# Hybrid decoder layer with 32 experts: w2 in packets of 16 KB, and three pieces of work moved

## The chip, the cores and the metric

The kernel runs on one core of a Trainium2 chip. Times are device microseconds of one execution, from launch to end; lower is better. The engines are PE (matrix products; PEld are its weight loads), DVE, ACT and POOL (work on vectors), and SP, which here only issues transfers.

## The reference

One layer on 256 rows of 1024 numbers, all in float32. First a mixing stage (a projection, differential attention beside an RWKV recurrence, an output projection), then a mixture of experts; each stage has its norms and takes shift, scale and gate from a conditioning vector. The attention needs a scalar `lambda` from four short vectors. The experts:

```python
logits = tok @ router_w + router_b
top_vals, top_idx = lax.top_k(logits, TOP_K)          # 4 of 32
gates = sum(one_hot(top_idx, 32) * softmax(top_vals)[..., None], axis=1)
...
out = clamped_swiglu(tok @ w1_e + b1_e) @ w2_e + b2_e   # w1_e 1024 x 2048, w2_e 1024 x 1024
acc = acc + g_e[:, None] * out                          # over all 32 experts
```

`clamped_swiglu` takes even and odd columns of its input as gate and linear part. All 32 experts' weights, 12 MB each, have to be read.

## The kernel before

The program is one function, in which the order of PE, DVE and ACT is mostly written out (under `manual_schedule`).

**Start (to about 60 us).** x is normed and transposed (`x_tr`), the shift and scale of the first 256 features come from two products of the conditioning vector with pieces of `ada_w` (`mod_rows`, copied by `mod_copy`, turned into columns by `mod_cols_first`), and `mod_x` makes the normed rows as a sum of two parts, high and low. `col_tr(0)` transposes small parameter rows into the columns `pc`. Seven matmuls with a tile of zeros clear the seven banks into which the first projection (`proj_first`) then accumulates. `warm(n)` issues n matmuls on ones whose result nobody reads. `shift` applies the token shift behind the projection. Lambda is four vectors' products, a sum, an Exp and a difference (L729 to L736). SP issues the loads in the order of the code; the table of the experts' first biases, `b1q` (128 rows of 512), is the last of `load_later` (L229) and is read by four matmuls and two splits about 230 us into the run.

**Middle (to about 240 us).** Attention, recurrence, output projection and router, in an order given by the string `WORK`.

**Experts (loop at L1923).** The experts are taken in an order by their number of rows; each has room for 64, 32 or 96 (`kind`). For expert p, `gemm1` (L1709) does 8 k-steps: the selected rows `xs[:, k]` are stationary, and 512 columns at a time of w1 move through PE, two or four streams in different column groups of PE (`parts`, L1684). `swiglu` makes `act` (DVE and ACT), `act_tr` transposes it, ACT copies it as `aTt`, and `gemm2` (L1736) does 8 k-steps with w2, each with a number of rows per partition. ACT and DVE evacuate the result as `ys`, and `scatter` (L1776) puts it back to the 256 rows by a product with the selection `back`; DVE adds it into `acc`. Work on the next expert (`gather`, `prep_back`, `gemm1_bias`) and the scatter of the previous one stand between these steps, some of it inside `gemm2` by the dictionary `between`, whose keys are k.

**Weights.** A ring of 18 slots of 1 MB holds them; an expert takes 8 for w1 and 4 for w2. `load_expert` (L1577) is a generator: one `next` behind each k-step of gemm1 issues a piece of the next expert, on SP's queue. w1 goes in four transfers of 2 MB, 16 KB (two rows) per partition, w2 in four of 1 MB, 8 KB (two rows) per partition, in the order `W2_ORDER`. The first four experts (`single`) take all of it in 1 MB.

**Last expert.** It has no successor. Its `between` (L1969) puts the scatter of the previous expert and `sum_so_far` (L1764: identity times `acc`, and the gates times the second biases `b2t`, into the four banks `ends`) into its gemm2, and 24 warm-up matmuls stand ahead of the transposes. The last `scatter` adds into `ends`, and `last_norm` and the output follow. `late_rows` (L1852) has POOL load the second biases at the start of the last expert.

Of the kernel before, what the change touches and what calls it, by code (L numbers as in the profile page):

```python
# [20 lines left out]
D = 1024  # L21
# [28 lines left out]
WARM = (34, 4, 0, 6, 8)  # L50
# [25 lines left out]
def hybrid_layer_kernel(ctx, tc, x, c, positions, ada_w, ada_b, pre_mix_norm, post_mix_norm,  # L76
# [146 lines left out]
    def load_later():  # L223
        for j, ap in enumerate((lam_q1, lam_k1, lam_q2, lam_k2)):
            nc.sync.dma_start(lamt[:, j], bcast(ap, [[0, 128], [1, 64]]))
        nc.sync.dma_start(rtw.rearrange("p (j r) e -> p j r e", r=2), router_w[0].rearrange(
            "(j p r) e -> p j r e", p=128, r=2))
        nc.sync.dma_start(rtb, router_b)
        nc.sync.dma_start(b1q, moe_b1[0].rearrange("e (q n) -> (e q) n", q=4))  # L229
# [68 lines left out]
    load_cols(0, S, ((("sh1", "sc1"), ada_b[0, 0:2 * D]), (("pre_mix",), pre_mix_norm[0])))  # L298
    ident = const.tile([128, 128], F32)
    V.tensor_scalar(ident, jp, 0.0, None, op0=OP.is_equal)  # L300

# [111 lines left out]
    norm_x(xj)  # L413
    x_tr(0, xj[0])
    mod_rows(0, 0, ada)
    x_tr(1, xj[1])
    mod_rows(0, 1, ada)
    col_tr(0)
# [8 lines left out]
    rwb = {}  # L427
    ORDER = (0, 2, 4, 6, 8, 10, 12)
    for f in ORDER:
        rwb[f] = (bankb if f in (12, 8, 10) else bank)()  # L430
        mm(rwb[f], zero, zero[:, 0:1].to_broadcast([128, 512]), True, False)
    warm(WARM[1], bankc)
# [11 lines left out]

    def shift(dst, p, f):
        S.activation(dst, p, AF.Copy, scale=mu1[:, f:f + 1])  # L446
        V.scalar_tensor_tensor(dst[:, 1:], p[:, 0:T - 1], col("mu", f), dst[:, 1:], op0=OP.mult, op1=OP.add)  # L447
# [281 lines left out]
    V.tensor_tensor(lamt[:, 0], lamt[:, 0], lamt[:, 1], op=OP.mult)  # L729
    V.tensor_tensor(lamt[:, 2], lamt[:, 2], lamt[:, 3], op=OP.mult)  # L730
    V.tensor_reduce(lam2, lamt[:, 0:4:2], axis=AX.X, op=OP.add)
    with tc.issue_after(first_act.ins):
        S.activation(lam2, lam2, AF.Exp)
    nlam = pro.tile([128, 1], F32)
    V.tensor_tensor(nlam, lam2[:, 1:2], lam2[:, 0:1], op=OP.subtract)
    V.tensor_scalar(nlam, nlam, LAMBDA_INIT, None, op0=OP.subtract)  # L736
# [416 lines left out]
    rkr, gB = rT, gT  # L1153
    fill()
# [422 lines left out]
    def load_expert(e, s1_, s2_, single=False):  # L1577


        w1 = moe_w1[0][e] if isinstance(e, int) else moe_w1[0][bass.ds(e, 1)].rearrange("o k n -> (o k) n")  # L1580
        w2 = moe_w2[0][e] if isinstance(e, int) else moe_w2[0][bass.ds(e, 1)].rearrange("o k n -> (o k) n")
        at = taken[0]
        taken[0] += KC + 4
        for j in range(4):

            d = ring[(at + 2 * j) % N_SLOTS // 2]
            s = w1[j * 256:(j + 1) * 256, :].rearrange("(p k) n -> p k n", k=2)
            s1_ += [d[:, 0], d[:, 1]]
            if j == 3:
                yield  # L1590
            if single:
                nc.sync.dma_start(d[:, 0], s[:, 0])
            if j == 3:
                yield
            if single:
                nc.sync.dma_start(d[:, 1], s[:, 1])
            else:
                nc.sync.dma_start(d.rearrange("p k n -> p (k n)"), s.rearrange("p k n -> p (k n)"))
        for n, k in enumerate(W2_ORDER):
            yield  # L1600
            s = s2_[k] = slot((at + KC + n) % N_SLOTS, (2, D))
            nc.sync.dma_start(s, w2[k * 256:(k + 1) * 256, :].rearrange("(p k) n -> p k n", k=2))
# [80 lines left out]

    def parts(bs, kind):  # L1684
        if kind != 32:
            for n in range(2):
                for h in range(2):
                    yield bs[n][64 * h:64 * h + 64], slice(0, 64), h * 1024 + n * 512
        if kind != 64:
            for q in range(4):  # L1690
                yield bs[-1][32 * q:32 * q + 32], slice(kind - 32, kind), q * 512
# [17 lines left out]
    def gemm1(bs, xs, w1s, kind, between=None, load=None):  # L1709
        for k in range(KC):  # L1710
            for o, s, c0 in parts(bs, kind):
                mm(o, xs[:, k, s], w1s[k][:, c0:c0 + 512], False, k == KC - 1)
# [21 lines left out]
    W2_ORDER = (0, 2, 1, 3)  # L1734

    def gemm2(aTt, w2s, gates_of, kind, between=None):  # L1736

        ks = [2 * s + j for s in W2_ORDER for j in range(2)]
# [37 lines left out]
    def scatter(ys, back, which=range(NT)):  # L1776
# [146 lines left out]
    for p in range(EXPERTS):  # L1923
        kind = kind_at(p)
        w1s, w2s = weights
        if p + 1 < EXPERTS:
            weights = [], {}
            rest_of_load = load_expert(expert_of(p + 1), *weights, p + 1 < SINGLE)
# [12 lines left out]
        if p + 1 < EXPERTS:  # L1941
# [16 lines left out]
            between[5] = lambda: back1.append(prep_back(nxt[1], gate1, kind1, picked(p + 1)))  # L1958
        back1 = []
        if p == 0:  # L1960
# [6 lines left out]
            between[3], between[5] = between[5], rest_of_first  # L1967
# [20 lines left out]
    scatter(*done[:2])  # L1988
# [67 lines left out]
```

## Time and profile before

| | us |
|---|---|
| three runs, lowest, median, highest | 1188.75, 1189.94, 1190.77 |
| the profiled execution, its own time | 1190.35 |
| its span, from first to last instruction | 1188.5 |
| PE busy in the span | 1078.3 (91%) |
| DVE, ACT busy | 412.1 (35%), 227.6 (19%) |
| DMA: moved, mean rate | 453.15 MB, 381 GB/s |
| mean granted clock of PE, as a share of full | 0.972 |

1.85 us of the execution lie outside the span. In the profile a busy PE may be waiting on its operands within a matmul; matmul ends are modelled. A row of a timeline is a start, a duration, engine and line, operation, what it writes <- what it reads, shape, count, and in brackets the idle time of its engine before it with what released it. Names are the program's, without numbers: `pair` is a slot of the ring (or, early on, a buffer in the same place), `bank`, `bankb`, `bankc` are accumulators. Line 104 is the helper behind every matmul, so matmuls are told apart by tiles. The chain of work that ended last is 45% transfers (44% weights of the experts) and 45% PE.

### The profile page before, as it was taken

The numbers are of one execution on the slowest core, as the hardware profiler recorded it, in microseconds if no ns is written. First come the engines' busy times: TensorE is split into PE (matmuls) and PEld (weight loads), VectorE is DVE, ScalarE is ACT, GpSimd is POOL, SyncE is SP. The second block draws the span as 40 slices with busy tenths as digits, with TensorE's granted clock in tenths as the row PEclk, the third lists the DMA queues.
The fourth block names the chain that finished last, engine by engine and source line by source line (L and its number), as shares of the span: only waits on it lengthen the run. The fifth ranks groups of instructions, "written<-read, shape, count | busy, mean of one in ns | idle before, by whom it ended". The sixth has DMA issues, their size and how long they took to land.

```text
span 1188.5 us, 17092 instructions
## 1 busy us (share of the span) xinstructions
PE 1078.3 (91%) x6717; PEld 507.3 (43%) x6717; DVE 412.1 (35%) x1114; ACT 227.6 (19%) x529; POOL 53.7 (5%) x100
## 2 busy tenths in 40 slices
PE   8999999999997877999988999988999999798765
PEld 6976667654343232233443233433333434333211
DVE  5688469852331212122323112312212223121203
ACT  4374353312011001010111010111010101101001
POOL 1331020000000000000000000000000000000000
PEclk8999999999999988999999999999999999999978
DMA  9862778899999999999999999999999999999991
GB/s 336 317 235 71 280 270 330 326 371 383 423 424 426 426 425 426 425 426 424 425 425 426 424 426 427 422 426 426 423 426 426 425 426 425 425 426 425 423 382 48
DMA packets 60101, 453.15 MB, mean 381 GB/s; under 512 B 7850, under 2 KB 16105, under 8 KB 23154
## 3 DMA queue, kind: packets, MB, share of 16 engines
q1 hardware_dynamic: 57970, 449.88, 91.9%
q0 software_dynamic: 1856, 2.13, 0.6%
q8 instruction: 54, 0.88, 0.3%
q14 instruction: 29, 0.24, 0.1%
q10 hardware_dynamic: 192, 0.02, 0.0%
HBM read 450.94 MB, written 1.06 MB: 380 GB/s over the span
## 4 chain that ended last, share of the span: by engine, by line
DMA 45%; PE 45%; DVE 6%; ACT 2%; issue 1%; SPq 0%; DVEq 0%; ACTq 0%
DMA pair<-in_moe_w 44%; PE bank L104 32%; PE bankb L104 10%; PE bankc L104 3%; DMA pair<-in_ada_w 1%; DVE pair L316 1%; PE bank L107 1%; ACT aTt L1731 0%; PE bankb L107 0%; DVE pair L447 0%; ACT xs L1656 0%; DVE w L316 0%; DVE pair L1195 0%; ACT pair L446 0%; DVE w L766 0%
## 5 line engine op out<-in xcount | busy, mean ns | idle before, releaser
L104 PE MATMUL bank<-pair,xs 128*64 128x512 f32 (+1 forms) x2240 | 408.6, 616 | 64.2 <-DMA pair<-in_moe_w 64.1
L104 PEld LDWEIGHTS bank<-pair,xs 128*64 128x64 f32 (+1 forms) x2240 | 114.5, 127 | 346.0 <-issue 241.3
L104 PE MATMUL bank<-pair,aTt 128*64 128x512 f32 (+1 forms) x1120 | 227.9, 618 | 12.0 <-ACT aTt L1731 10.7
L1676 DVE TENSOR_SCALAR glu<-bank 128x256 f32<-128x256 f32 x55 | 23.1, 420 | 397.2 <-PE bank L104 397.1
L1679 ACT ACTIVATE act<-glu 128x256 f32<-128x256 f32 x55 | 22.9, 417 | 464.8 <-DVE glu L1676 464.8
L1789 DVE TENSOR_TENSOR acc<-acc,bankb 128x512 f32<-128x512 f32 x120 | 77.4, 681 | 94.6 <-PE bankb L104 94.6
L104 PEld LDWEIGHTS bank<-pair,aTt 128*64 128x64 f32 (+1 forms) x1120 | 53.2, 126 | 124.9 <-issue 101.2
L104 PEld LDWEIGHTS bankb<-sel,own 128*128 128x128 f32 x608 | 73.5, 198 | 14.7 <-DVE glu L1676 9.0
L104 PE MATMUL bankb<-sel,own 128*128 128x96 f32 (+3 forms) x608 | 76.4, 285 | 0.0
L1759 ACT ACTIVATE ys<-bank,gs 128x512 fp32r<-128x512 f32 x32 | 22.0, 687 | 261.2 <-PE bank L104 261.2
L1760 DVE SCALAR_TENSOR_TENSOR ys<-bank,gs,ys 128x512 fp32r<-128x512 f32 x32 | 24.0, 751 | 106.2 <-ACT ys L1759 106.2
L104 PE MATMUL bankb<-ys,back 64*128 64x512 f32 x254 | 55.8, 449 | 4.7 <-DVE acc L1789 3.5
L1656 ACT ACTIVATE xs<-bankb,s2c,g2c 128x128 f32<-128x128 f32 (+2 forms) x136 | 48.3, 436 | 42.4 <-PE bankb L104 42.4
L1651 DVE TENSOR_SCALAR back<-bankb,pcol 128x256 fp32r<-128x256 f32 x35 | 16.6, 483 | 87.6 <-PE bankb L104 87.6
L104 PEld LDWEIGHTS bankb<-ys,back 64*128 64x128 f32 x254 | 25.8, 191 | 42.3 <-issue 26.0
L104 PE MATMUL bankb<-w,w 128*128 128x512 f32 (+3 forms) x120 | 30.9, 366 | 0.0
L1731 ACT ACTIVATE aTt<-bank 128x256 f32<-128x256 f32 x55 | 19.2, 386 | 50.6 <-PE bank L107 50.4
L104 PE MATMUL bankb<-w,own 128*128 128x512 f32 x80 | 27.3, 424 | 0.0
L104 PE MATMUL bank<-own,pair 128*128 128x256 f32 x128 | 26.6, 293 | 0.0
L104 PE MATMUL bank<-pair,pair 32*32 32x32 f32 (+4 forms) x400 | 26.1, 246 | 0.1
L104 PE MATMUL bankc<-pair,cs 128*32 128x256 f32 (+1 forms) x256 | 24.6, 493 | 1.4 <-DMA pair<-in_ada_w 1.4
L107 PE MATMUL bank<-ident,act 128*128 128x128 f32 x110 | 22.4, 315 | 2.4 <-DVE act L1681 2.4
(482 smaller groups left out, 1011.0 us busy)
## 6 DMA issues: line engine op xcount, KB each, us to landing
pair<-in_moe_w SPq DMA_DIRECT2D x112, 2048.0 KB
pair<-in_moe_w SPq DMA_DIRECT2D x160, 1024.0 KB
pair<-in_ada_w SPq DMA_DIRECT2D x24, 1024.0 KB
pair<-in_w_in SPq DMA_DIRECT2D x8, 896.0 KB
pair<-in_w_in SPq DMA_DIRECT2D x6, 1024.0 KB
pair<-in_w_out SPq DMA_DIRECT2D x4, 1024.0 KB
own<-in_x SPq DMA_DIRECT2D x2, 512.0 KB
own<-in_x SPq DMA_DIRECT2D x1, 1024.0 KB
```

The costliest lines, as they stand in the source:

```text
L104: PE.matmul(o, l, r, start=start, stop=stop)
L107: PE.transpose(o, i, ident[0:i.shape[0], 0:i.shape[0]])
L316: last_lo = lo_eng.tensor_tensor(lo, src, hi.bitcast(F32), op=OP.subtract)
L1651: V.tensor_scalar(back[:, j], b3, pcol32[:, j:j + 1] if j or kind == 32 else pcol64, None, op0=OP.is_equal)
L1656: S.activation(xs[:, k, :cap], b, AF.Identity, scale=g2c[:, k:k + 1], bias=s2c[:, k:k + 1])
L1676: V.tensor_scalar(glu, v[:, :, 0], 7.0, None, op0=OP.min)
L1679: S.activation(dst, glu, AF.Tanh, scale=0.851)
L1731: S.activation(aTt[:, j0:j0 + 2], b[:, :256].rearrange("p (a b) -> p a b", a=2), AF.Copy)
L1759: S.activation(yh, b, AF.Copy, scale=gs[:, j:j + 1])
L1760: V.scalar_tensor_tensor(yl, b, gs[:, j:j + 1], yh.bitcast(F32), op0=OP.mult, op1=OP.subtract)
L1789: V.tensor_tensor(a, a, b, op=OP.add)
```

## The change

It has seven parts.

1. w2 goes in two transfers of 2 MB, 16 KB (four rows) per partition. The first four experts and the last keep pieces of 1 MB, the last MB of the last expert comes as two of 512 KB.
2. w2's rows now lie four to a partition, so `act` must come in another order: `gemm1` reads w1 in runs of four columns, of which every second run belongs to one stream. The first biases are permuted the same way: `b1q` is loaded at the start on ACT's queue, four matmuls with a table of ones and zeros (`ztile`) reorder it ahead of the first transposes, and ACT copies it back.
3. `col_tr(0)` stands behind the first half of the transposes.
4. Four of the seven matmuls that clear banks stand ahead of `mod_cols_first`, three behind it, and the four warm-up matmuls are gone.
5. Lambda's operations stand behind the last shift of the projection.
6. In the last expert both `sum_so_far` and the scatter of the previous expert stand in its gemm1, behind k = 1, 3 and 5. The scatter goes straight into `ends`, so DVE's four additions into `acc` fall away. 10 warm-up matmuls replace 24.
7. w2's pieces are used in their natural order; keys of `between` are renumbered.

```diff
-WARM = (34, 4, 0, 6, 8)
+WARM = (34, 10, 0, 6, 8)
...
-        nc.sync.dma_start(b1q, moe_b1[0].rearrange("e (q n) -> (e q) n", q=4))
...
+    S.dma_start(b1q, moe_b1[0].rearrange("e (q n) -> (e q) n", q=4))
...
+    ztile = w4s(2, 2, 128)
+    V.memset(ztile, 0.0)
+    for n in range(4):
+        V.tensor_copy(ztile[:, n // 2, n % 2, n % 2:128:2], ident[:, n // 2:128:2])
...
     norm_x(xj)
+
+    bp = bankb()
+    for q in range(2):
+        for n in range(2):
+            mm(bp[:, q * 256:(q + 1) * 256], ztile[:, q, n],
+               b1q.rearrange("q (m n f) -> q n m f", n=2, f=4)[:, n], not n, n == 1)
     x_tr(0, xj[0])
+    col_tr(0)
     mod_rows(0, 0, ada)
+    S.activation(b1q, bp, AF.Copy)
     x_tr(1, xj[1])
     mod_rows(0, 1, ada)
-    col_tr(0)
+    rwb = {}
+    ORDER = (0, 2, 4, 6, 8, 10, 12)
+
+    def clear(*fs):
+        for f in fs:
+            rwb[f] = (bankb if f in (12, 8, 10) else bank)()
+            mm(rwb[f], zero, zero[:, 0:1].to_broadcast([128, 512]), True, False)
+
+    clear(*ORDER[:4])
...
     mod_cols_first(0)
-    rwb = {}
-    ORDER = (0, 2, 4, 6, 8, 10, 12)
-    for f in ORDER:
-        rwb[f] = (bankb if f in (12, 8, 10) else bank)()
-        mm(rwb[f], zero, zero[:, 0:1].to_broadcast([128, 512]), True, False)
-    warm(WARM[1], bankc)
+    clear(*ORDER[4:])
...
+    later.enter_context(tc.issue_after(last_shift.ins))
+    V.tensor_tensor(lamt[:, 0], lamt[:, 0], lamt[:, 1], op=OP.mult)
...
-    def load_expert(e, s1_, s2_, single=False):
+    def load_expert(e, s1_, s2_, single=False, last=False):
...
-        for n, k in enumerate(W2_ORDER):
-            yield
-            s = s2_[k] = slot((at + KC + n) % N_SLOTS, (2, D))
-            nc.sync.dma_start(s, w2[k * 256:(k + 1) * 256, :].rearrange("(p k) n -> p k n", k=2))
+        for j in range(2):
+
+            d = ring[(at + KC + 2 * j) % N_SLOTS // 2]
+            s = w2[j * 512:(j + 1) * 512, :].rearrange("(p k) n -> p k n", k=4)
+            for h in range(2):
+                s2_[2 * j + h] = view(d[:, h], (2, D))
+                yield
+                if single or last:
+
+                    for n in range(2) if last and j and h else (slice(0, 2),):
+                        nc.sync.dma_start(s2_[2 * j + h][:, n], s[:, 2 * h:2 * h + 2][:, n])
+                elif h:
+                    nc.sync.dma_start(d.rearrange("p k n -> p (k n)"), s.rearrange("p k n -> p (k n)"))
...
-                    yield bs[n][64 * h:64 * h + 64], slice(0, 64), h * 1024 + n * 512
+                    yield bs[n][64 * h:64 * h + 64], slice(0, 64), h, n
...
         for k in range(KC):
-            for o, s, c0 in parts(bs, kind):
-                mm(o, xs[:, k, s], w1s[k][:, c0:c0 + 512], False, k == KC - 1)
+            w = w1s[k].rearrange("p (h m n f) -> p h n m f", h=2, n=2, f=4)
+            for o, s, h, n in parts(bs, kind):
+                mm(o, xs[:, k, s], w[:, h, n], False, k == KC - 1)
...
-                        mm(ends[i][n], back[h, j, i], y[h], False, m == len(ys) - 1)
+                        mm(ends[i][n], back[h, j, i], y[h], False, last and m == len(ys) - 1)
...
+        if p == EXPERTS - 1:
+            between = {1: lambda: sum_so_far(0), 3: lambda: sum_so_far(1), 5: lambda: scatter(*done[:2])}
         gemm1(bs, xs, w1s, kind, between, rest_of_load)
...
         elif not nxt:
-            warm(24)
-            between = {0: lambda: scatter(*done[:2], which=(0,)), 1: lambda: scatter(*done[:2], which=(1,)),
-                       5: lambda: sum_so_far(0), 3: lambda: sum_so_far(1)}
+            warm(WARM[1])
+            between = {}
...
-    scatter(*done[:2])
+    scatter(*done[:2], last=True)
```

What this does to the order of instructions is shown at three places. First SP's queue, the weights of an expert in the middle (`pair_...` are slots; 128x4096 is 2 MB, 128x2048 is 1 MB; ISA are register steps for the expert's address). Before:

```order
L1598 ISA
L1598 DMA pair_2699<-in_moe_w 128x4096
L1598 ISA
L1598 DMA pair_1427<-in_moe_w 128x4096
L1602 ISA
L1602 DMA pair_1159<-in_moe_w 128x2048
L1602 ISA
L1602 DMA pair_1159<-in_moe_w 128x2048
L1602 ISA
L1602 DMA pair_578<-in_moe_w 128x2048
L1602 ISA
L1602 DMA pair_578<-in_moe_w 128x2048
```

And now:

```order
L1619 ISA
L1619 DMA pair_2706<-in_moe_w 128x4096
L1619 ISA
L1619 DMA pair_1434<-in_moe_w 128x4096
L1632 ISA
L1632 DMA pair_1166<-in_moe_w 128x4096
L1632 ISA
L1632 DMA pair_586<-in_moe_w 128x4096
```

Four transfers of w2 have become two of twice the size. Second PE's queue at the end, the last expert from its transposes to its last scatter (`pair_1159` and `pair_578` are w2, `pair_776` the second biases). Before:

```order
L107 MATMUL bank<-ident,act 128x128 x2
L104 MATMUL bank<-pair_1159,aTt 32x512 x2
L104 MATMUL bankb<-ys,back 128x512 x4
L104 MATMUL bank<-pair_1159,aTt 32x512 x2
L104 MATMUL bankb<-ys,back 128x512 x4
L104 MATMUL bank<-pair_1159,aTt 32x512 x4
L104 MATMUL bankb<-acc,ident 128x512
L104 MATMUL bankb<-pair_776,pgT 128x512
L104 MATMUL bankb<-acc,ident 128x512
L104 MATMUL bankb<-pair_776,pgT 128x512
L104 MATMUL bank<-pair_578,aTt 32x512 x4
```

Now the same work stands among the products with w1 (`pair_2704` to `pair_1434`, of which `pair_2705` and `pair_2706` are the second and third 2 MB):

```order
L104 MATMUL bank<-pair_2704,xs 32x512 x8
L104 MATMUL bankb<-acc,ident 128x512
L104 MATMUL bankb<-pair_783,pgT 128x512
L104 MATMUL bankb<-acc,ident 128x512
L104 MATMUL bankb<-pair_783,pgT 128x512
L104 MATMUL bank<-pair_2705,xs 32x512 x8
L104 MATMUL bankb<-acc,ident 128x512
L104 MATMUL bankb<-pair_783,pgT 128x512
L104 MATMUL bankc<-acc,ident 128x512
L104 MATMUL bankc<-pair_783,pgT 128x512
L104 MATMUL bank<-pair_2706,xs 32x512 x8
L104 MATMUL bankb<-ys,back 128x512 x6
```

Behind the transposes there are now two groups of eight products with w2 and the final scatter, and nothing between. (A float32 product shows as one row here and as two instructions in the trace.) Third PE's queue at the start, from the transposes of x to the column products. Before:

```order
L107 MATMUL bank<-ident,pair_174 128x128 x8
L104 MATMUL bankc<-pair_87,cs 32x256 x8
L107 MATMUL bank<-ident,pair_174 128x128 x8
L104 MATMUL bankc<-pair_89,cs 32x256 x8
L107 MATMUL bankb<-ident,prow_85 128x24
L104 MATMUL bankc<-q_115,w_221 128x1 x4
```

Now:

```order
L104 MATMUL bankb<-b1q,w_129 128x256 x4
L107 MATMUL bank<-ident,pair_181 128x128 x8
L107 MATMUL bankb<-ident,prow_85 128x24
L104 MATMUL bankc<-pair_87,cs 32x256 x8
L107 MATMUL bank<-ident,pair_181 128x128 x8
L104 MATMUL bankc<-pair_89,cs 32x256 x8
L104 LDWEIGHTS zero
L104 MATMUL bank<-zero 128x512
```

The table's four products come first, the parameter rows (`prow_85`) move ahead, and clearing starts ahead of the column products (`q_115`).

## Rows read from the trace of the kernel before

**Rows 1.** The page's 40 slices: GB/s that the DMA engines moved, 29.7 us each.

```profile
GB/s 336 317 235 71 280 270 330 326 371 383 423 424 426 426 425 426 425 426 424 425 425 426 424 426 427 422 426 426 423 426 426 425 426 425 425 426 425 423 382 48
```

**Rows 2.** Window: us, busy PE, PEld, DVE, ACT, POOL, granted clock, DMA share, GB/s.

```profile
360.00:1110.00 750.00, 687.86 (x3769) 268.28 (x3771) 178.41 (x412) 91.59 (x223) 9.61 (x27) 0.98 1.01 425
```

**Rows 3.** Timeline of SP's queue: start, duration, line, what it issues, count.

```profile
361.82 15.03 SPq L1598 DMA_DIRECT2D pair<-in_moe_w  x4
379.01 7.78 SPq L1602 DMA_DIRECT2D pair<-in_moe_w  x4
391.36 15.01 SPq L1598 DMA_DIRECT2D pair<-in_moe_w  x4
```

**Rows 4.** SP's waits: us in total, times, longest.

```profile
SPq L1598 <- DMA pair<-in_moe_w: 371.4, 96, 5.7
```

**Rows 5.** Timeline of PE, last expert; idle time before in brackets.

```profile
1137.24 3.64 PE L104 MATMUL bank<-pair,xs 128*32 128x512 f32 x16 [4.28 <-DMA pair<-in_moe_w]
1142.15 3.45 PE L104 MATMUL bank<-pair,xs 128*32 128x512 f32 x16 [1.27 <-DMA pair<-in_moe_w]
1147.04 1.92 PE L104 MATMUL bank<-pair,xs 128*32 128x512 f32 x16 [1.44 <-DMA pair<-in_moe_w]
1151.93 3.53 PE L104 MATMUL bank<-pair,xs 128*32 128x512 f32 x16 [2.96 <-DMA pair<-in_moe_w]
...
1159.00 1.05 PE L104 MATMUL bank<-pair,aTt 128*32 128x512 f32 x4 [0.53 <-ACT aTt L1731]
1159.98 0.74 PE L104 MATMUL bankb<-ys,back 64*128 64x512 f32 x4
...
1163.30 1.12 PE L104 MATMUL bankb<-acc,ident 128*128 128x512 f32 x2
...
1167.51 1.06 PE L104 MATMUL bank<-pair,aTt 128*32 128x512 f32 x8
...
1172.72 1.06 PE L104 MATMUL bank<-pair,aTt 128*32 128x512 f32 x8
```

**Rows 6.** Windows in the last expert, columns as in rows 2.

```profile
1136.00:1140.00 4.00, 2.76 (x16) 0.60 (x16) 0.00 (x0) 0.00 (x0) 0.00 (x0) 0.50 0.99 422
...
1144.00:1148.00 4.00, 2.56 (x24) 0.42 (x20) 0.00 (x0) 0.00 (x0) 0.00 (x0) 0.84 1.01 428
...
1160.00:1162.00 2.00, 2.00 (x14) 0.73 (x12) 1.25 (x2) 0.00 (x0) 0.00 (x0) 1.00 0.14 53
```

**Rows 7.** Timeline of POOL: issue of the experts' second bias rows.

```profile
1122.68 0.53 POOL L1860 DMA_DIRECT2D pair<-in_moe_b  x1 [0.73 <-PE bank L104]
```

**Rows 8.** The DMA view's issues: the same load, KB and us to landing.

```profile
pair<-in_moe_b POOLq DMA_DIRECT2D x1, 128.0 KB, 12.8
```

**Rows 9.** Timeline of weight loads: every second number, then neighbours.

```profile
617.59 7.61 PEld L104 LDWEIGHTS bankb<-sel,own 128*128 128x128 f32 x64 [0.81 <-DVE glu L1676]
...
651.47 0.97 PEld L104 LDWEIGHTS bankb<-pgS,sel 128*128 128x128 f32 x8
```

**Rows 10.** Timeline of PE at the start.

```profile
8.70 1.09 PE L107 MATMUL bank<-ident,pair 128*128 128x128 f32 x8 [1.73 <-DVE pair L347]
...
15.69 1.84 PE L104 MATMUL bankc<-q,w 128*128 128x1 f32 x8 [1.16 <-DVE w L375]
...
20.33 1.06 PE L104 MATMUL bankc<-ones 128*128 128x256 bf16 x4
21.04 0.56 PE L104 MATMUL bank<-own,pair 128*128 128x256 f32 x1
```

**Rows 11.** Instructions on the tile b1q: durations in ns, first start in us.

```profile
L315 ACT ACTIVATE b1h<-b1q x1: 630/630/630, 236.5 to 236.5; 128x512 fp32r<-128x512 f32 x1
```

**Rows 12.** Timeline of DVE: the first of lambda's operations.

```profile
70.66 0.21 DVE L729 TENSOR_TENSOR lamt<-lamt 128x64 f32<-128x64 f32 x1
```

**Rows 13.** Groups of PE by shape: gemm1's matmuls, busy us, mean ns.

```profile
L104 PE MATMUL bank<-pair,xs 128*64 128x512 f32 x1280 | 288.9, 599 | 23.6 <-DMA pair<-in_moe_w 23.6
...
L104 PE MATMUL bank<-pair,xs 128*32 128x512 f32 x960 | 122.8, 638 | 40.5 <-DMA pair<-in_moe_w 40.5
```

More of the change, by code (lines that the diff above doesn't have):

```diff
@@ L443, in hybrid_layer_kernel @@
     mu1 = pro.tile([128, 14], F32)
+    last_shift = None
     def shift(dst, p, f):
-        S.activation(dst, p, AF.Copy, scale=mu1[:, f:f + 1])
+        nonlocal last_shift
+        last_shift = S.activation(dst, p, AF.Copy, scale=mu1[:, f:f + 1])
         V.scalar_tensor_tensor(dst[:, 1:], p[:, 0:T - 1], col("mu", f), dst[:, 1:], op0=OP.mult, op1=OP.add)
@@ L728, in hybrid_layer_kernel @@
     lam2 = pro.tile([128, 2], F32)
[L729 to L733, printed above, removed]
     nlam = pro.tile([128, 1], F32)
-    V.tensor_tensor(nlam, lam2[:, 1:2], lam2[:, 0:1], op=OP.subtract)
-    V.tensor_scalar(nlam, nlam, LAMBDA_INIT, None, op0=OP.subtract)
     sub_c = pro.tile([128, 1], F32)
@@ L1153, in hybrid_layer_kernel @@
     rkr, gB = rT, gT
+    later = ExitStack()
+    later.enter_context(tc.issue_after(last_shift.ins))
+    V.tensor_tensor(lamt[:, 0], lamt[:, 0], lamt[:, 1], op=OP.mult)
+    V.tensor_tensor(lamt[:, 2], lamt[:, 2], lamt[:, 3], op=OP.mult)
+    V.tensor_reduce(lam2, lamt[:, 0:4:2], axis=AX.X, op=OP.add)
+    S.activation(lam2, lam2, AF.Exp)
+    V.tensor_tensor(nlam, lam2[:, 1:2], lam2[:, 0:1], op=OP.subtract)
+    V.tensor_scalar(nlam, nlam, LAMBDA_INIT, None, op0=OP.subtract)
+    later.close()
     fill()
@@ L1687, in parts @@
                 for h in range(2):
-                    yield bs[n][64 * h:64 * h + 64], slice(0, 64), h * 1024 + n * 512
+                    yield bs[n][64 * h:64 * h + 64], slice(0, 64), h, n
         if kind != 64:
             for q in range(4):
-                yield bs[-1][32 * q:32 * q + 32], slice(kind - 32, kind), q * 512
+                yield bs[-1][32 * q:32 * q + 32], slice(kind - 32, kind), q // 2, q % 2
     def gemm1_bias(oneh, kind):
@@ L1732, in act_tr @@
         return aTt
-    W2_ORDER = (0, 2, 1, 3)
     def gemm2(aTt, w2s, gates_of, kind, between=None):
-        ks = [2 * s + j for s in W2_ORDER for j in range(2)]
+        ks = range(KC)
         b64 = bank() if kind != 32 else None
@@ L1774, in hybrid_layer_kernel, with scatter @@
     summed = set()
-    def scatter(ys, back, which=range(NT)):
+    def scatter(ys, back, which=range(NT), last=False):
         for i in which:
@@ L1927, in hybrid_layer_kernel @@
             weights = [], {}
-            rest_of_load = load_expert(expert_of(p + 1), *weights, p + 1 < SINGLE)
+            rest_of_load = load_expert(expert_of(p + 1), *weights, p + 1 < SINGLE, p + 2 == EXPERTS)
             next(rest_of_load)
@@ L1957, in hybrid_layer_kernel @@
                 bs = gemm1_bias(onehot(p + 1), kind1)
-            between[5] = lambda: back1.append(prep_back(nxt[1], gate1, kind1, picked(p + 1)))
+            between[3] = lambda: back1.append(prep_back(nxt[1], gate1, kind1, picked(p + 1)))
         back1 = []
@@ L1965, in rest_of_first @@
                 back = prep_back(sel_, gate0, 64, picked(0))
-            between[3], between[5] = between[5], rest_of_first
+            between[1], between[3] = between[3], rest_of_first
         elif not nxt:
-            warm(24)
-            between = {0: lambda: scatter(*done[:2], which=(0,)), 1: lambda: scatter(*done[:2], which=(1,)),
-                       5: lambda: sum_so_far(0), 3: lambda: sum_so_far(1)}
+            warm(WARM[1])
+            between = {}
         elif not early:
```

## The prediction

> **What bounds the kernel now.** I read the page's slices first, then a window of the middle, then the queue that issues the transfers, then the two ends. The slices [rows 1] split the kernel in two: in the first ten, of some 30 us each, the DMA rate is uneven; from the eleventh on it stands at 422 to 427 GB/s until the last two. In the window from 360 to 1110 us [rows 2] the DMA share is 1.01 at 425 GB/s while PE is busy 687.86 of 750 us: PE has 62 us to spare there and the transfers have none. SP's own rows say the same [rows 3]: it issues one expert in 29.54 us (361.82 to 391.36), and at the line of w1's transfers alone it waited 371.4 us for an earlier transfer to land [rows 4]. So for most of the run only bytes and the pace of a transfer count. At the end this turns over: the last weights land, and PE still has work.
>
> **Last expert's sums (the tail).** PE's rows of the last expert [rows 5]: its four w1 transfers start PE at 1137.24, 1142.15, 1147.04 and 1151.93, 4.90 us apart, with PE idle before each. The weights of w2 follow: four of 1 MB at 2.48 us each (the pace is worked out below) put the last landing at 1151.93 + 9.93 = 1161.86, and the windows agree: 53 GB/s between 1160 and 1162 is 0.1 MB, the last of it [rows 6]. Yet the last matmuls of gemm2 begin at 1172.72 and end at 1173.78. In the 14.78 us from its first at 1159.00 to there lie the eight sums (1163.30 to 1167.51, and the same again: 8.4 us), eight matmuls of the scatter (0.74 us for each four, 1.3 us where they overlap their neighbours), and two k-steps that run alone in 1.05 us each, where two side by side take 1.06 (1.0 us lost). The change takes all of it out of gemm2: 14.78 - 10.7 leaves 4.1 us, an end at 1163.1; landing plus one k-step alone gives 1161.86 + 1.05 = 1162.9. I take 1163.0, a gain of **10.8 us**; the ends are 10.6 and, if the split of the last MB lets its final half finish early and the act chain comes sooner by the shorter warm-up, 11.5. Behind gemm2 nothing changes: evacuation, final scatter, norm and output run 14.7 us to the span's end either way.
>
> Where the removed work goes: into the idle time in front of w1's later transfers. There PE waits 1.27, 1.44 and 2.96 us [rows 5], 5.7 us together, and the work is 4 sums (2.1 us) after k=1, 4 sums after k=3, 8 scatter matmuls (1.3 us) after k=5, at full clock 5.5 us. It fits only at full clock. The granted clock there was 0.50 in 1136 to 1140, the lower level (1.2 GHz), and 0.84 on average in 1144 to 1148 [rows 6], after PE had waited 4.28 us and then worked in pieces. With the sums in the gaps PE works through from 1137.24: k=0,1 to 1140.9, sums to 1143.5 (half of them still at the lower level), k=2,3 to 1145.4, sums to 1147.5, k=4,5 to 1149.5, scatter to 1150.8; the last w1 at 1151.93 finds PE free, and its 16 matmuls then take 1.92 us as at 1147.04, not the 3.53 that they took at 1151.93. So the act chain would not be late, and the landing sets the end. The sums need the bias rows that POOL loads: issued at 1122.68 [rows 7], 12.8 us to landing [rows 8], there at 1135.5, wanted at 1140.9.
>
> **Larger packets of w2.** 27 of 32 experts change from four transfers of 1 MB to two of 2 MB; four early ones and the last keep theirs. SP issues four w1 transfers in 15.03 us and four of w2 in 7.78 [rows 3], three steps and one issue (about 0.34 us by the difference to three steps of 4.90): 4.90 us per 2 MB of w1 and 2.48 per 1 MB of w2, so 0.07 us more per 2 MB in small packets, 0.13 per expert. The period gives 29.54 - 4 x 4.90 - 2 x 4.90 = 0.16 per expert. Times 27 that is 3.5 to 4.2 us; I take **3.8**. Bounds: nothing, if the difference belongs to something else; and 6.0, if all of the stretch went at w1's pace (2.097 MB in 4.90 us is 428 GB/s against 425 [rows 2]: 750 x 3/428 = 5.3 us on 25.4 of the 27 experts, 5.6 on all, rounded up). It lies wholly on the path, since the transfers are what the stretch waits for. Issuing 2 MB one k-step later costs nothing while eight transfers are under way.
>
> The Trainium skill speaks against this part ("DMA: Bandwidth & Descriptors", section "Why small descriptors are slow"): a packet has a fixed cost of about 3 cycles, and joining packets is worth it only at 256 bytes or less. By that figure 8 KB packets, 256 beats of 32 bytes, lose 1.2%, half of which would return: an estimate of 0.06 us per expert, 1.6 us in all, and the sum would be 1177.0. The trace shows about twice that difference between the two sizes, and nothing yet of w2 in 16 KB; that packets give less is the first rival.
>
> **Strided reads in gemm1.** To match the new row order gemm1 reads runs of four numbers and skips four. Cost in no row of before. The nearest row: 64 weight loads of every second number take 7.61 us, 0.119 each, and eight of neighbouring numbers 0.97, 0.121 each [rows 9]. From this I take 0. A loss would have to use up PE's 62 us first.
>
> **Front.** PE's first projection matmul starts at 21.04 [rows 10], and the work behind it follows without a wait for long, so what is removed before it moves everything. Gone: the idle 1.16 us before the shift and scale columns at 15.69 (four of the seven zero matmuls move into it, the column transpose goes earlier), and the four warm-up matmuls at 20.33, 0.7 us until the next start [rows 10]. Against this: four matmuls of the bias table ahead of the transposes, some 1.1 us if they go like the four warm-up matmuls of that width (1.06), in part in the 1.73 us that PE waits for the norm at 8.70; its 256 KB, early now, at 336 GB/s [rows 1] 0.78 us by which the first weights come later; and a copy on ACT between two evacuations, 0.6 us by the copy of the same table later [rows 11]. The five small lambda operations on DVE (0.21 us for the first [rows 12], 0.9 at most for all) leave a place between the projection's shifts. I take **0.5 us gained**; ends: 2.8 gained (1.16 + 0.7 + 0.9) and 2.5 lost (1.1 + 0.78 + 0.6). The permuted table replaces the same four loads later; nothing waits there.
>
> **Sum.** 1190.35 - 10.8 - 3.8 - 0.5 = 1175.25 us against the profiled execution, which stands 0.4 above the median of the three runs: 1174.8.
>
> **Rivals.**
> 1. The packets' size gives nothing, because the pace is the bytes': the 0.07 us would belong to the slots that w2 goes to or to what else is under way. For it: 425 GB/s is already within 1% of w1's 428. Against: SP's pace and the period both show w2 slower [rows 3], in one and the same stretch. Time 1174.8 + 3.8 = 1178.6; if a part of the 3.8 comes, between the two. Chance 0.15.
> 2. The sums delay the last w1: the clock stays at the lower level. Then from 1137.24 on 3.64 + 4.2 + 3.6 + 4.2 + 3.6 + 2.6 + 3.6 us, gemm1 ends at 1162.7, not at 1151.93 + 3.53; with 3.6 us to gemm2 and 4.2 there the end is 1170.5, 7.5 us later than forecast: 1182.3. For it: 0.50 in the very stretch. Against: it had risen by 1144 to 1148 after two pieces of 3.5 us with a wait of 1.27 between, and the waits now are filled. Chance 0.10.
> 3. Slower than before: the strided operand slows gemm1, in all 32 experts. Its matmuls are busy 288.9 + 122.8 = 411.7 us [rows 13]. Up to 62/411.7, 15% slower, the transfers hide it (19% if only those of the stretch count, 328 us); beyond about 20 to 24% it has eaten the gains too. At double time it costs 411.7 - 62 = 350 us: about 1525. For it: four streams of 512 columns read at once in the kind of 32 rows; against: the weight loads of every second number. Chance 0.07.
> 4. The front loses its 2.5 us (bias table late, PE waiting ahead of the transposes) and nothing else differs: 1174.8 + 3.0 = 1177.8. Chance 0.04.
>
> **Numbers.** The forecast keeps 0.64. About 2.4 us (0.2%) is what a measurement of this kernel can tell from no change. Every case but the third gains at least 7 us, so faster is 0.92, the same 0.01, slower 0.07. The range runs from 1169 (tail 11.5, packets 6.0, front 2.8) to 1182.4 (the second rival); only the third and remainders lie outside.
>
> **What would show it.** Right: gemm2's last matmul about 11 us nearer to the last w1; no sums behind it; in the last gemm1 the clock at 1.00 before k=6; an expert's period on SP of 29.4 instead of 29.54; gemm1's mean time per matmul as before; first projection matmul at about 20.5. Wrong: the period unchanged (rival 1), idle before the last w1 gone and act late (2), DMA share under 1 in the middle (3).

## The result and the profile after

| | before | changed |
|---|---|---|
| median of four runs, us | 1190.24 | 1175.16 |
| lowest to highest, us | 1188.75 to 1190.77 | 1173.14 to 1177.38 |
| profiled execution, us | 1190.35 | 1175.14 |
| its span, us | 1188.5 | 1173.4 |

The ratio is 0.9876, with a 95% interval of 0.9861 to 0.9891: 14.8 us less, 13.0 to 16.5. The forecast was 1174.8. Three executions further below took 1540.89, 1560.54 and 4643.66 us and are left out of the medians there.

Three marks split both profiled executions: the start of the first expert's first matmul, of the last expert's first matmul, and the end of the last gemm2.

| us | front, to first expert | middle, to last expert | last expert, to end of gemm2 | rest of span |
|---|---|---|---|---|
| before | 242.18 | 895.06 | 36.54 | 14.75 |
| changed | 241.20 | 891.48 | 25.62 | 15.07 |
| less by | 0.98 | 3.58 | 10.92 | -0.32 |

With 0.05 outside the span that is the 15.21 us between the two profiled executions. The forecast had 0.5, 3.8 and 10.8.

**The tail.** PE's timeline of the changed kernel in the last expert, against [rows 5]:

```profile
1132.68 2.81 PE L104 MATMUL bank<-pair,xs 128*32 128x512 f32 x16 [4.22 <-DMA pair<-in_moe_w]
1135.42 1.89 PE L104 MATMUL bankb<-acc,ident 128*128 128x512 f32 x2
...
1140.40 1.92 PE L104 MATMUL bank<-pair,xs 128*32 128x512 f32 x16
1142.25 1.13 PE L104 MATMUL bankb<-acc,ident 128*128 128x512 f32 x2
...
1146.46 1.92 PE L104 MATMUL bank<-pair,xs 128*32 128x512 f32 x16
1148.32 0.97 PE L104 MATMUL bankb<-ys,back 64*128 64x512 f32 x5
...
1149.46 1.92 PE L104 MATMUL bank<-pair,xs 128*32 128x512 f32 x16
...
1154.29 4.01 PE L104 MATMUL bank<-pair,aTt 128*32 128x512 f32 x32 [0.53 <-ACT aTt L1763]
```

Only the first matmul waits for a weight. The sums and the scatter fill what was idle between the w1 pieces, and more: the second four sums alone take 4.21 us (1142.25 to 1146.46). Gemm2 is one block of 4.01 us where it was 14.78, and its start does not wait for a transfer. The clock and the transfers in this stretch (columns as in [rows 2]), against [rows 6]:

```profile
1132.00:1136.00 4.00, 3.32 (x17) 0.98 (x18) 0.00 (x0) 0.00 (x0) 0.00 (x0) 0.70 1.02 434
1136.00:1140.00 4.00, 4.00 (x8) 0.88 (x6) 0.00 (x0) 0.00 (x0) 0.00 (x0) 0.88 0.97 414
1140.00:1144.00 4.00, 4.00 (x22) 1.01 (x20) 0.00 (x0) 0.00 (x0) 0.00 (x0) 1.00 1.01 426
```

After the wait of 4.22 us the clock fell below full for a while; it was at 1.00 from 1140 on and stayed there: the last w1 piece takes 1.92 us, where it took 3.53 before [rows 5].

**The middle.** SP's timeline of the changed kernel, against [rows 3]: one expert from 380.31 to 409.65 is 29.34 us, where it was 29.54, and w2 is two issues.

```profile
380.31 15.01 SPq L1619 DMA_DIRECT2D pair<-in_moe_w  x4
399.84 5.23 SPq L1632 DMA_DIRECT2D pair<-in_moe_w  x2
409.65 15.01 SPq L1619 DMA_DIRECT2D pair<-in_moe_w  x4
```

The middle window of the changed kernel: 427 GB/s against 425 [rows 2].

```profile
360.00:1100.00 740.00, 678.85 (x3735) 266.38 (x3729) 176.89 (x405) 90.89 (x222) 9.60 (x27) 0.98 1.01 427
```

Gemm1's matmuls by shape, against [rows 13]: 599 ns as before, and 623 against 638 in the other shape, which is the last expert's clock.

```profile
L104 PE MATMUL bank<-pair,xs 128*64 128x512 f32 x1280 | 288.7, 599 | 20.9 <-DMA pair<-in_moe_w 20.8
...
L104 PE MATMUL bank<-pair,xs 128*32 128x512 f32 x960 | 119.5, 623 | 34.9 <-DMA pair<-in_moe_w 34.9
```

**The front.** PE's timeline of the changed kernel at the start, against [rows 10]:

```profile
10.62 3.64 PE L104 MATMUL bankb<-b1q,w 128*128 128x256 f32 x8 [4.36 <-DMA b1q<-in_moe_b]
14.09 1.04 PE L107 MATMUL bank<-ident,pair 128*128 128x128 f32 x8
...
19.13 1.05 PE L104 MATMUL bankc<-q,w 128*128 128x1 f32 x8
...
21.39 0.38 PE L104 MATMUL bank<-own,pair 128*128 128x256 f32 x1 [0.53 <-ACT own L399]
```

PE waits 4.36 us for the table, the transposes of x start at 14.09 in place of 8.70, and the first projection is 0.35 us later than before, not earlier. Before's own 21.04 stands behind some 5 us at the lower clock:

```profile
16.00:18.00 2.00, 2.00 (x10) 1.65 (x10) 0.41 (x3) 0.61 (x2) 1.27 (x1) 0.50 1.03 357
18.00:20.00 2.00, 2.00 (x6) 0.70 (x5) 1.70 (x4) 1.92 (x5) 0.72 (x1) 0.50 1.12 351
20.00:22.00 2.00, 2.00 (x10) 1.54 (x9) 1.90 (x4) 1.67 (x2) 0.86 (x1) 0.50 1.09 357
```

Yet the experts start 0.98 us earlier. Comparing the two timelines row by row puts the whole of that between 100 and 104 us, in work that the change does not touch. The windows there, of before and then of the changed kernel:

```profile
100.00:102.00 2.00, 1.93 (x10) 1.71 (x10) 2.00 (x4) 0.40 (x1) 0.00 (x0) 0.70 0.00 0
102.00:104.00 2.00, 2.00 (x6) 1.41 (x6) 2.00 (x5) 0.20 (x1) 0.95 (x1) 0.50 0.55 142
```

```profile
100.00:102.00 2.00, 1.93 (x12) 1.59 (x13) 2.00 (x4) 0.54 (x1) 0.00 (x0) 1.00 0.00 0
102.00:104.00 2.00, 1.78 (x13) 1.33 (x12) 2.00 (x4) 0.35 (x2) 0.95 (x1) 1.00 0.61 128
```

In that execution of before the clock fell to the lower level for these matmuls, which cost it 1.15 us. Without that the fronts would have been 0.17 us apart, the changed one slower. So three questions went to the chip: is the middle's gain the packets, is the tail's gain the sums, and what is the front worth?

### The profile page after: what moved, and what is told of

Its sections match the earlier page's. It is cut to its first block, busy times and chain, and to the rows that moved or that the text cites. A ratio compares the mean times of both kernels' runs of the same rounds, so it can differ in the third digit from the quotient of the medians.

```text
span 1173.4 us, 16844 instructions
## 1 busy us (share of the span) xinstructions
PE 1066.7 (91%) x6706; PEld 503.9 (43%) x6707; DVE 409.2 (35%) x1115; ACT 227.7 (19%) x530; POOL 52.9 (5%) x100
## 4 chain that ended last, share of the span: by engine, by line
PE 56%; DMA 33%; DVE 6%; ACT 2%; issue 1%; SPq 0%; ACTq 0%; DVEq 0%
PE bank L104 41%; DMA pair<-in_moe_w 31%; PE bankb L104 12%; PE bankc L104 2%; DMA pair<-in_ada_w 1%; PE bank L107 1%; DVE pair L321 1%; DMA b1q<-in_moe_b 1%; DMA lamt<-in_da_lambda_q 1%; ACT aTt L1763 1%; PE bankb L107 0%; ACT xs L1686 0%; DVE w L321 0%; DVE pair L1216 0%; DVE act L1711 0%
## 5 line engine op out<-in xcount | busy, mean ns | idle before, releaser
L104 PE MATMUL bank<-pair,aTt 128*64 128x512 f32 (+1 forms) x1120 | 223.0, 606 | 14.3 <-ACT aTt L1763 10.7
L1819 DVE TENSOR_TENSOR acc<-acc,bankb 128x512 f32<-128x512 f32 x116 | 74.9, 682 | 89.6 <-PE bankb L104 89.6
```

The source lines that it names most:

```text
L104: PE.matmul(o, l, r, start=start, stop=stop)
L1819: V.tensor_tensor(a, a, b, op=OP.add)
```

## The experiments

Each time below is a median, and the ratio, with its 95% interval, is to the kernel before on the same chip. Before's median was 1187.84 us on the chip of the first four experiments, 1188.55 on that of every fourth number, the old front, the longer warm-up and both variants, and 1190.23 on that of the others. Single runs of one kernel spread by 3 us and more, so what is small is read from the marks of the profiled executions as well.

**The change once more.**

> The changed kernel once more, beside the others on one chip. Expected 1175 us, within 1.5 of it. In its first profile one stretch of the kernel before (about 100 to 104 us) had the lower clock (0.50) and cost that execution 1.15 us that the changed one did not lose; the theory is that this belongs to the execution and not to the change, so that at 230 us the two differ by under 0.3 us when both have the same clock there. The rival is that the moved operations of the front remove it: then this run has it removed again and every run with the old front has it.

Measured: 1175.9 us, ratio 0.9918 (0.9889 to 0.9947). By the ratio that is 9.7 us less than before, 6.3 to 13.2, where the first measurement had 14.8; two of the seven executions took 1184 us, no kernel before was profiled on this chip, and what made up the difference is open. The tail is 25.90 us and the middle 891.34, as in the first profile. The front is not: the experts start at 238.78, 2.42 us earlier than in the first profile of the same kernel. PE's timeline of this run:

```profile
9.89 1.96 PE L104 MATMUL bankb<-b1q,w 128*128 128x256 f32 x8 [2.97 <-DVE turns L557]
11.69 1.04 PE L107 MATMUL bank<-ident,pair 128*128 128x128 f32 x8
...
18.98 0.38 PE L104 MATMUL bank<-own,pair 128*128 128x256 f32 x1 [0.53 <-ACT own L399]
```

The same eight instructions on the table took 3.64 us in the first profile and 1.96 here. The windows from 10 to 16 us, of the first profile and of this run, show why:

```profile
10.00:12.00 2.00, 1.38 (x3) 1.18 (x4) 0.75 (x2) 0.00 (x0) 0.00 (x0) 0.65 1.09 371
12.00:16.00 4.00, 4.00 (x31) 2.92 (x29) 0.63 (x5) 1.27 (x3) 0.00 (x0) 0.75 1.06 413
```

```profile
10.00:12.00 2.00, 2.00 (x11) 1.74 (x12) 0.46 (x1) 0.00 (x0) 0.00 (x0) 1.00 1.08 359
12.00:16.00 4.00, 4.00 (x49) 2.42 (x48) 2.36 (x17) 2.66 (x5) 0.00 (x0) 1.00 1.06 414
```

The experts start 3.40 us earlier than before's 242.18, and 1.15 of that is 100 to 104 us. That does not yet answer my expectation of under 0.3 us at equal clock: ahead of the projection the clock was at 1.00 here and at 0.50 in before. The profiles under "The old front on the new rest" answer it.

**w2 in 1 MB transfers, 8 KB packets.**

```diff
-                if single or last:
+                if True:
```

> The change with w2 of all experts in pieces of 1 MB, 8 KB per partition, all else as changed. If 16 KB packets are what gained in the middle, an expert's period grows by 0.13 to 0.16 us and the time by about 3.6 us over the change's, to about 1178.8 us. If packets don't matter (first rival) the time stays within 1 us of the change's.

Measured: 1177.92 us, ratio 0.9926 (0.9899 to 0.9952), against 1175.9 of the change on the same chip. The times alone do not settle 3.6 us; the middle does: 895.41 us, as before's 895.06.

**w2 in 2 MB transfers, 8 KB packets.** The rows of w2 come in another order than act's columns.

```diff
-                    nc.sync.dma_start(d.rearrange("p k n -> p (k n)"), s.rearrange("p k n -> p (k n)"))
+                    nc.sync.dma_start(d, w2[j * 512:(j + 1) * 512, :].rearrange("(h p k) n -> p h (k n)", h=2, k=2))
```

> The change with w2 in the same two transfers of 2 MB, but each as two pieces of 8 KB per partition (w2's rows then stand in another order than act's columns; the amount of work is the same). If the size of a packet is what gained, this loses the same 3.6 us as with 1 MB transfers, to about 1178.8 us. If the number of transfers is, it stays at the change's 1175 us.

Measured: 1178.53 us, ratio 0.9919 (0.9899 to 0.9939); middle 895.46. The number of transfers was the change's, the packets before's, and the gain is gone. The middle window of this run is back at 425 GB/s:

```profile
360.00:1100.00 740.00, 679.49 (x3712) 265.49 (x3709) 175.46 (x403) 90.91 (x222) 9.60 (x27) 0.98 1.01 425
```

All profiles together, but for that of every fourth number: with 8 KB packets the middle took 895.06, 895.66, 895.41 and 895.46 us; with 16 KB it took 891.48, 891.34, 892.00, 891.45, 891.35, 890.78, 892.04, 892.33 and 891.80. The means are 895.40 and 891.62, so packets are worth 3.8 us, and the two groups do not overlap. It is the size of the packet, not of the transfer. The packets in before's trace point the same way: from 360 to 1100 us one of 8 KB took 313.9 ns in the mean and one of 16 KB 616.8, so two small ones take 11.0 ns more than a large one.

**The sums back in gemm2.**

```diff
-            between = {1: lambda: sum_so_far(0), 3: lambda: sum_so_far(1), 5: lambda: scatter(*done[:2])}
...
-            warm(WARM[1])
-            between = {}
+            warm(24)
+            between = {0: lambda: scatter(*done[:2], which=(0,)), 1: lambda: scatter(*done[:2], which=(1,)),
+                       3: lambda: sum_so_far(0), 5: lambda: sum_so_far(1)}
```

> The change with the sums and the scatter of the last expert back between the steps of its gemm2, and 24 warm-up matmuls. If the tail's 10.8 us came from there, the time is 10 to 11.5 us over the change's, about 1186 us. If the gain at the end came from the landing (the split last MB, an earlier act) the loss is under 5 us.

Measured: 1186.85 us, ratio 1.0002 (0.9981 to 1.0023), 11 us over the change. Its tail is 36.48 us, before's 36.54. The split last MB stayed in and changes nothing there. This kernel kept the packets and the front, some 4 us by the forecast; its marks show them against before's one profile (240.85 and 892.00), but its times, within 2.7 us of before's either way, do not.

**Only the sums, in the kernel before.** Part 6 of the change alone, on the old kernel.

> The kernel before with only the last expert's sums and scatter moved into its gemm1 (and 10 warm-up matmuls). By the forecast's term 10.8 us less than before: about 1179.3 us. By the rival that the lower clock holds the last gemm1 back: 3 us less, about 1187 us.

Measured: 1178.09 us, ratio 0.9897 (0.9878 to 0.9917): 12.3 us less than before's 1190.23 on its chip, 9.9 to 14.5. Its tail is 25.60 us. With the experiment above this gives the part from both sides.

**The scatter in place of the warm-up.**

```diff
-            between = {1: lambda: sum_so_far(0), 3: lambda: sum_so_far(1), 5: lambda: scatter(*done[:2])}
+            between = {1: lambda: sum_so_far(0), 3: lambda: sum_so_far(1)}
...
-            warm(WARM[1])
+            scatter(*done[:2])
```

> The change with the last expert's scatter of its predecessor taken out of gemm1 and put in place of the ten warm-up matmuls, where PE waits for act anyway. In the change PE came to the last w1 2.1 us after it had landed. Expected: act 1.4 us earlier, gemm2 ends 1.0 us earlier, bounded by the last landing: about 1174.1 us. If the landing bounds already, no difference.

Measured: 1176.29 us, ratio 0.9887 (0.9869 to 0.9905); tail 25.62 us, unchanged. PE's timeline:

```profile
1144.64 1.93 PE L104 MATMUL bank<-pair,xs 128*32 128x512 f32 x16 [0.66 <-DMA pair<-in_moe_w]
...
1149.48 1.92 PE L104 MATMUL bank<-pair,aTt 128*32 128x512 f32 x16 [0.53 <-ACT aTt L1763]
1152.01 1.07 PE L104 MATMUL bank<-pair,aTt 128*32 128x512 f32 x8 [0.61 <-DMA pair<-in_moe_w]
1153.26 1.05 PE L104 MATMUL bank<-pair,aTt 128*32 128x512 f32 x4 [0.19 <-DMA pair<-in_moe_w]
1154.50 1.05 PE L104 MATMUL bank<-pair,aTt 128*32 128x512 f32 x4 [0.18 <-DMA pair<-in_moe_w]
```

Here w1's last piece and each later piece of w2 are waited for: PE came to gemm2 earlier and got nothing for it. From the last expert's first w1 piece on, 25.6 us is the transfers' time to the last landing plus one k-step; the change sits on that bound, with PE's own chain close behind it. Where the clock came back later at the start of the last gemm1, the chain set the end: 25.90 us in the change's second profile and 26.25 in that with the table later. What I expected, 1 us, was not there to gain.

**Gemm1 on every second number, and on every fourth.** The hidden columns and the first biases then do not belong together; the amount of work is the same.

```diff
-            w = w1s[k].rearrange("p (h m n f) -> p h n m f", h=2, n=2, f=4)
+            w = w1s[k].rearrange("p (h m n f) -> p h n m f", h=2, n=2, f=1)
```

> The change with gemm1 reading every second number of w1 instead of runs of four (the hidden columns and the first biases then don't belong together; the amount of work is the same). If a strided operand costs PE something, it shows here: mean time of gemm1's matmuls over 599 ns (kind of 64 rows) and 623 ns (32 rows), and above 15 to 19% more also the time. If strides are free, both as in the change and 1175 us.

Measured: 1177.05 us, ratio 0.9884 (0.9856 to 0.9912). Matmuls by shape:

```profile
L104 PE MATMUL bank<-pair,xs 128*64 128x512 f32 x1280 | 300.0, 616 | 6.8 <-DMA pair<-in_moe_w 6.8
...
L104 PE MATMUL bank<-pair,xs 128*32 128x512 f32 x960 | 124.6, 645 | 25.7 <-DMA pair<-in_moe_w 25.7
```

So this stride is not free: gemm1 is busy 424.6 us against 408.2, 4% more. No time follows, since PE has idle time to give; its waits for weights in the first shape fell from 20.9 to 6.8 us.

```diff
+            w = w1s[k].rearrange("p (m n) -> p n m", n=4)
...
-                mm(o, xs[:, k, s], w[:, h, n], False, k == KC - 1)
+                mm(o, xs[:, k, s], w[:, 2 * h + n], False, k == KC - 1)
```

> The change with gemm1 reading every fourth number of w1 (columns of the hidden layer then don't belong together; the amount of work is the same). Every second number cost gemm1 616 against 599 ns per matmul in the kind of 64 rows. If what counts is how many of the four numbers in 16 bytes are used, this costs more: over 616 ns, perhaps double 599, and then the time grows beyond 1190 us. If a stride as such costs the 3%, it stays at 616 and the time at 1175 us.

Measured: 1513.45 us, ratio 1.2718 (1.2638 to 1.2798). Matmuls by shape, then the middle window:

```profile
L104 PE MATMUL bank<-pair,xs 128*64 128x512 f32 x1280 | 584.6, 1079 | 0.0
L104 PE MATMUL bank<-pair,xs 128*32 128x512 f32 x960 | 223.9, 1079 | 0.0
```

```profile
360.00:1100.00 740.00, 728.79 (x2836) 202.76 (x2828) 132.22 (x301) 67.86 (x166) 7.33 (x21) 0.99 0.81 321
```

Gemm1's busy time doubles (808.5 against 408.2 us), nothing waits for weights any more, and the DMA share falls to 0.81. The price follows the third rival's formula: 400 us more, less the 62 us that PE had to spare, is 338, and 1513.45 - 1175.16 is 338. That it fits to the unit is luck: PE still idles 11 us in this window, and the two times are from different chips. The rival was a real mechanism; runs of four just do not trigger it.

**The table's matmuls later.** All of it behind the second `mod_rows`, the seven clearing matmuls behind the column products.

```diff
     x_tr(1, xj[1])
     mod_rows(0, 1, ada)
+    bp = bankb()
+    for q in range(2):
+        for n in range(2):
+            mm(bp[:, q * 256:(q + 1) * 256], ztile[:, q, n],
+               b1q.rearrange("q (m n f) -> q n m f", n=2, f=4)[:, n], not n, n == 1)
...
-    clear(*ORDER[4:])
+    clear(*ORDER)
```

> The change with the four matmuls on the bias table moved behind the second part of the modulation's rows, and all seven clearing matmuls behind the column products. In the change PE waits 4.36 us for the table's load ahead of the transposes of x. If that wait costs time, the first projection matmul comes at about 19 us instead of 21.39 and the experts about 2 us earlier: 1173 us. If the front is bound by its transfers, the projection starts earlier and nothing is left of it at 60 us: 1175 us.

Measured: 1174.48 us, ratio 0.9871 (0.9851 to 0.9891). PE's timeline:

```profile
8.71 1.09 PE L107 MATMUL bank<-ident,pair 128*128 128x128 f32 x8 [1.35 <-DVE pair L352]
...
14.71 1.99 PE L104 MATMUL bankb<-b1q,w 128*128 128x256 f32 x8
...
18.91 0.38 PE L104 MATMUL bank<-own,pair 128*128 128x256 f32 x1
```

The wait for the table is gone, the projection comes at 18.91 and the experts at 238.92. That is where the change's own second profile has them, also at full clock (18.98 and 238.78). So the wait costs nothing by itself; it was the lower clock in the first profile that cost 2 us.

**The old front on the new rest.** The table loaded where it was and not permuted, so the first biases stand in the wrong columns; transposes, clearing, warm-up and lambda as before.

> The change with the front of the kernel before: table loaded late on SP and not permuted (so the first biases stand in the wrong order of columns), column transposes, clearing, four warm-up matmuls and lambda where they were. By the forecast's term 0.5 us over the change. By the profiles so far: first projection matmul at about 20.9 us, against 19.0 (clock at full rate) or 21.2 (a stretch at 0.5 between 10 and 16 us) in the change, so 0 to 2 us over the change, 176 to 1177 after 1000. If the early table costs more than the rest gives, it is faster than the change.

(The last figures mean 1176 to 1177 us.) Measured: 1174.54 us, ratio 0.9866 (0.9820 to 0.9913), against 0.9876 and 0.9918 of the change in its two measurements: the times show no gain from the front. The start of the experts in all profiles with the old front (three) and with the changed one (eight), by where the clock fell on the way there:

| us | nowhere | ahead of the projection | there, and at 100 to 104 us |
|---|---|---|---|
| old front | | 240.31 | 242.18, 242.42 |
| changed front | 238.78, 238.98, 239.15, 239.20 | 240.78, 240.85, 241.20 | 242.25 |

Where the clock fell at the same places (not always for as long), the changed front is 0.5 to 0.9 us later in the one column and within 0.2 us in the other: the new order by itself shows no gain. What differs is the clock ahead of the projection. All three old fronts lost it, after PE had worked in pieces (in before it was busy 2.06 of the 4 us from 12 to 16); four of the eight changed ones kept it, and that is worth about 2 us. Whether the change makes that likelier, so few profiles do not show, and the times do not either. The fall at 100 to 104 us belongs to neither front: one old front is without it and one changed front has it.

**A longer warm-up at the start.** `WARM = (60, 10, 0, 6, 8)`.

> The change with 60 in place of 34 warm-up matmuls at the very start, so that PE works instead of waiting until the table lands. If the wait of 2.4 to 4.4 us ahead of the table is what brings the lower clock between 10 and 16 us in some executions, that stretch keeps the full clock and the first projection matmul comes at about 19.0 us. If the clock falls there all the same, it comes at 21 us and the wait is not the cause.

Measured: 1179.67 us, ratio 0.9907 (0.9872 to 0.9942). In its one profile PE waits 0.18 us for the table, the clock is 1.00 from 8 to 24 us and the projection comes at 19.42, near the 19.0 expected. But one profile proves no cause: the change's second profile waited 2.97 us at the same place and kept the clock, and the run with 2 MB transfers of 8 KB lost it after 2.44. Without the long wait, here and in the two profiles with the table later, the clock was kept each time; with it, in four of eight. The execution was long for another reason, further on, where before's clock is 1.00 in all three windows; its experts start at 253.06:

```profile
130.00:150.00 20.00, 18.62 (x225) 12.73 (x224) 3.32 (x4) 6.34 (x14) 0.78 (x2) 0.83 0.69 259
150.00:170.00 20.00, 18.35 (x313) 12.09 (x312) 10.13 (x22) 9.88 (x25) 7.34 (x14) 0.91 0.66 254
170.00:190.00 20.00, 20.00 (x129) 13.18 (x128) 9.83 (x24) 7.88 (x24) 0.00 (x0) 0.58 0.63 207
```

**Both variants together**, the table later and the scatter for the warm-up.

> Both variants together: the table's matmuls behind the modulation's rows, the last expert's scatter in place of the warm-up. Expected about 1173.5 us, 1 us under the change at most, since gemm2's end hangs on the last landing; if the front's transfers bound the start, equal to the change.

Measured: 1175.56 us, ratio 0.9896 (0.9837 to 0.9954); front 239.57, middle 892.33, tail 25.64. Equal to the change; no version here beats it by what can be measured.

## Why the prediction was right, point by point

- **Which stretch is bound by what.** Right. The middle gained only what the transfers gained (427 GB/s against 425, DMA share 1.01 in both), and 62 us of PE's spare time hid a gemm1 that was 4% slower.
- **The tail, 10.8 us.** Right in size: 10.92 in the first profile, and 11 and 12 us by the two runs that take it out and put it in alone. One step of it failed: "the last w1 at 1151.93 finds PE free". PE came to that piece at 1149.46, while the first piece's 1132.68 plus three steps of 4.90 is 1147.4, so 2 us late. The term that was wrong is the price of the sums there: the prediction books four at 2.1 us, though by its own rows, and in the tail's sum, four take 4.2 (8.4 for eight), and 4.21 is what the second four took at full clock. So 9.7 us of work, not 5.5, went into 5.7 us of idle time. At full clock the three pieces, eight sums and the scatter take 15.1 us, 0.4 more than the three steps of 4.90; the lower clock at their start made it 16.8. The 2 us cost nothing measurable in this profile, because gemm2 then needed no transfer and took 4.01 us in one block, so that the size came out right with that error in it. The run with the scatter moved shows the other limit: a PE that is earlier waits for the landing.
- **The packets, 3.8 us.** Right: 3.58 in the first profile, 3.8 by the means of thirteen. The first rival is out, by the run with large transfers and small packets. The Trainium skill's rule ("DMA: Bandwidth & Descriptors", section "Why small descriptors are slow") gave an estimate of 1.6 us by its figure of about 3 cycles per packet, and advised joining only at 256 bytes or less. The trace differs: going from 8 to 16 KB saved 27 x 256 / 16 = 432 packets on each DMA engine and 3.8 us, 8.8 ns for each packet. The measurement decides: joining was worth it at 8 KB, because the transfers were the bound.
- **Strided reads, 0.** Right for runs of four (599 ns in both). The row that I took it from was a poor witness: weight loads of every second number cost nothing, while a moving operand of every second number costs 4%, and of every fourth doubles gemm1. The Trainium skill ("SBUF — State Buffer", the note on cachelines under "Door 1: The DMA port swizzle") speaks of lines of 16 bytes and full bandwidth from two hits in a line. The traces agree at four hits (no cost) and at one (a price, here double), and differ at two: 616 against 599 ns.
- **The front, 0.5 us.** Within its bounds by luck, and not understood when forecast: the 0.98 of the first profiles is 1.15 us of lower clock in before at 100 to 104 us, less 0.17 lost. The wait for the table was 4.36 us, not the part of 1.73 that the forecast hid it in, and the table's four matmuls take 1.96 us at full clock and 3.64 here, not 1.1; the work behind caught up all but 0.35 us. The row that the 1.1 and the 0.7 came from, the warm-up at 20.33 [rows 10], is bf16 where the table is float32, and it ran at 0.50, which the prediction did not look at. What moves the front by 2 us is the clock ahead of the projection: when it is kept, the changed order gets there at 19.0 to 19.3, otherwise at 21.0 to 21.4.
- **The second rival (lower clock in the last gemm1).** In part there: 0.70 in 1132 to 1136, 0.88 to 1140, full from then on. That cost 1.7 us of the 7.5, off the path in the first profile; in the second the tail was 0.28 us longer. The rival's own price was too low in one term: the 4.2 us that it books for four sums at the lower level is what they take at full clock.
- **What was not forecast.** The rest of the span behind gemm2 grew by 0.32 us. It is 14.68 to 14.75 us in the three kernels that load all of w2 in 1 MB transfers and 15.06 to 15.16 in the others. The last output transfer is issued 10.05 us behind gemm2's end in before and 10.04 in the changed kernel, so the 0.3 us lie behind the work, at the end of the program; why is open.

## What to carry to other kernels

Where the profile shows one stretch at DMA share 1.01, cost an edit there in packets and bytes alone, and put other work into PE's idle time there. At the end of a kernel, compare the last landing with the last matmul: what lies between can move ahead of the landing, as far as PE's idle time there holds it, and it is worth its whole duration until the landing binds. Price it there with the same row as where it is taken out. Before a row becomes a term of a sum, read the granted clock beside it. A moving operand of float32 may be read in runs of four numbers, 16 bytes, at no cost (599 ns); shorter runs have a price that the bound may hide.

## What the runs showed of the hardware that was not expected

- At full load a packet costs something beyond its bytes, even at 8 KB: going to 16 KB gave 8.8 ns for each packet spared per engine, and 2 MB transfers of 8 KB packets gave nothing.
- A moving operand of float32 read at every second number made gemm1 4% longer, at every fourth 98% longer (408.2, 424.6 and 808.5 us busy).
- The clock falls below full (1.2 in place of 2.4 GHz) for short stretches in one execution and not in the next of the same kernel: at 10 to 14 us it cost 1.7 us on eight instructions. Between two kernels with the same work there, it cost 1.15 us at 100 to 104 us, and in one run 14 us between 130 and 190. Two profiles can therefore differ by a microsecond or more in a place that nobody changed; comparing the timelines row by row, with the clock beside them, tells this from an effect.
